# Attention on one core: scaling of two heads of four moved to ScalarE, and one tile per key block for the transposed probabilities

## The chip, the cores and the metric

The kernel runs on one core of a Trainium2 chip. The core has five engines that run their own instruction streams and wait for one another by semaphores: TensorE (PE in the profile; PEld is its loading of weights), VectorE (DVE), ScalarE (ACT), GpSimd (POOL) and SyncE (SP, which issues the DMAs). SBUF is the on-chip memory of 128 partitions; PSUM holds what TensorE writes. The metric is the device time of one execution in microseconds, the median of the runs.

## The reference, cut to what matters

The program is a block of a diffusion transformer: 512 latent tokens and 256 context tokens of width 1024, two layers. Each layer has a mixer (attention, a convolution and a state-space scan side by side, one output projection) and an MLP. Only the attention is touched by the change. It has 8 query heads in 2 groups of 4 (one group for each key head, `kv`), width 64. A block of 128 latent tokens sees itself and its two neighbours, all 256 context tokens, and a "sink" logit that takes part in the sum of the softmax and has no value:

```python
s_lat = jnp.where(mask, jnp.einsum('bqhgd,bkhd->bhgqk', qb, kb) * scale, NEG_INF)
s_ctx = jnp.einsum('bqhgd,bkhd->bhgqk', qb, kc) * scale
p = jax.nn.softmax(jnp.concatenate([s_lat, s_ctx, s_sink], axis=-1), axis=-1)
out = einsum('bhgqk,bkhd->bqhgd', p_lat, vb) + einsum('bhgqk,bkhd->bqhgd', p_ctx, vc)
```

Context tokens attend to the context alone, and only in the first layer (layer 0), since the second layer (layer 1) has no context output.

## The kernel before, in words

All large products are float32 products made of three passes on TensorE (`mm3`, L640 to L642: high by high, high by low, low by high part), so a weight that comes by DMA is split first, by a cast on ScalarE (L623) and a subtraction on VectorE or GpSimd (L624).

The attention stage is `phase_a`. After keys, values and queries it walks over units. A unit is one tile of 128 tokens and one `kv`, that is four heads. Layer 0 has 12 units: four of context tokens with 2 key blocks (256 columns of scores), then eight of latent tokens, the first and the last two with 4 key blocks (512 columns), the other four with 5 (640 columns). Layer 1 has the eight latent units alone. For each unit:

- `attn_scores`: for each of the four heads TensorE makes the scores (L932 to L935) in a PSUM tile `ps_q` (two buffers), and VectorE adds the mask and takes the maximum while it writes them to an SBUF tile `p` (L936). Then small steps on VectorE (L940, L941), the exponential of the sink on ScalarE (L942), the exponential of each head on ScalarE with the row sum beside it (L944), the sum and its reciprocal on VectorE (L946, L947), and at last the scaling of each head's `p` by the reciprocal: four instructions on VectorE (L949).
- `attn_values`: for each key block `j` TensorE transposes that block of the four heads (L962) into one PSUM tile `ps_t` (two buffers, shared by the transposes, the products with the values and the query transposes L905). The block is copied to SBUF, into `pts`, by ScalarE for even `j` (L569 is the line of the helper `E.copy`) and by VectorE for odd `j` (L963). `pts` is one tile for all blocks of a unit, with one buffer. Then the products with the values (L969, two for each block), a cast of the result on ScalarE (L972) and a subtraction on VectorE (L973) into the tiles that the output projection reads.

`values` of a unit is written one unit behind its `scores`. Between units TensorE gets other work: query transposes for the next units (L905, with L910 and L911 behind them) and the first pass of the output projection (`pass0`, copied by ScalarE at L1357, multiplied by GpSimd at L1359). After the attention comes `phase_post` with the second pass, the normalisation (L587 to L606, L732) and the modulation before the MLP (L782 to L787).

What sets the order: the kernel is written with a tile framework that is told `schedule_with_timeline_sim=True`. It simulates the engines and sets the order of each engine's instructions by its simulated times. So an edit of an instruction's engine or of a tile's buffers changes the order of others too, also away from the edit. On the chip each engine then runs its stream strictly in that order.

Of the kernel before, what the change touches and what calls it, by code (L numbers as in the profile page):

```python
# [7 lines left out]
F32 = mybir.dt.float32  # L8
# [4 lines left out]
OP = mybir.AluOpType  # L13
AX = mybir.AxisListType

P = 128
# [898 lines left out]
def attn_scores(E, blk, kv, qs, lat, kt):  # L915

    nc = E.nc
    V = nc.vector
    keys = ([k for k in (blk - 1, blk, blk + 1) if 0 <= k < 4] if lat else []) + [4, 5]
    nk = len(keys)  # L920
    nl = nk - 2
    moff = {0: 1, 1: 0, 2: 0, 3: 5}[blk] if lat else 3
    p = [E.p3([P, 5 * P]) for _ in range(4)]
    st = E.sm.tile([P, 4, 4], F32, name="st", tag="st", bufs=4)
    mx, nm, sm, es = (st[:, k] for k in range(4))
    for i in range(4):
        pq = E.pt('q')
        l0 = 512 - nl * P
        qi = qs[:, i // 2, i % 2]
        if nl:  # L930
            rk = slice(keys[0] * P, (keys[0] + nl) * P)
            nc.tensor.matmul(pq[:, l0:512], qi, kt[0][:, kv, rk], start=True, stop=False)  # L932
            nc.tensor.matmul(pq[:, l0:512], qi, kt[1][:, kv, rk], start=False, stop=True)
        nc.tensor.matmul(pq[:, 512:768], qi, kt[0][:, kv, NL:], start=True, stop=False)
        nc.tensor.matmul(pq[:, 512:768], qi, kt[1][:, kv, NL:], start=False, stop=True)  # L935
        V.tensor_tensor_reduce(out=p[i][:, :nk * P], in0=pq[:, l0:768],  # L936
                               in1=E.mask[:, moff:moff + nk].rearrange("p a b -> p (a b)"), scale=0.125,
                               scalar=-3e38, op0=OP.add, op1=OP.max, accum_out=mx[:, i:i + 1])
    h4 = slice(kv * 4, kv * 4 + 4)
    V.scalar_tensor_tensor(out=nm, in0=mx, scalar=-1.0, in1=E.nsink[:, h4], op0=OP.mult, op1=OP.min)  # L940
    V.tensor_sub(es, nm, E.nsink[:, h4])  # L941
    nc.scalar.activation(es, es, AF.Exp)  # L942
    for i in range(4):
        nc.scalar.activation(p[i][:, :nk * P], p[i][:, :nk * P], AF.Exp, bias=nm[:, i:i + 1],  # L944
                             accum_out=sm[:, i:i + 1])
    V.tensor_add(sm, sm, es)  # L946
    V.reciprocal(sm, sm)  # L947
    for i in range(4):
        V.tensor_scalar(out=p[i][:, :nk * P], in0=p[i][:, :nk * P], scalar1=sm[:, i:i + 1], scalar2=None,  # L949
                        op0=OP.mult)  # L950
    return p, keys


def attn_values(E, kv, p, keys, v, mix):
    nc = E.nc
    V = nc.vector
    nk = len(keys)
    pts = E.ap.tile([P, 5, 512], F32, name="pts", tag="pts", bufs=1)
    for j in range(nk):
        pt = E.pt('t')  # L960
        for i in range(4):
            nc.tensor.transpose(pt[:, i * P:(i + 1) * P], p[i][:, j * P:(j + 1) * P], E.ident)  # L962
        (V.tensor_copy if j % 2 else E.copy)(pts[:, j], pt)  # L963
    po = E.pt('t')
    for j in range(nk):
        vv = v[:, keys[j], kv * 64:(kv + 1) * 64]
        pr = pts[:, j].rearrange("p (a e t) -> p a e t", a=2, e=2)
        for e in range(2):
            nc.tensor.matmul(po[e * 64:(e + 1) * 64, :256], vv, pr[:, :, e], start=j == 0, stop=j == nk - 1)  # L969
    pv = po[:, :256].rearrange("p (a t) -> p a t", a=2)  # L970
    mh, ml = mix(0), mix(1)
    nc.scalar.copy(mh, pv)  # L972
    V.tensor_sub(ml, pv, mh.bitcast(F32))  # L973
# [275 lines left out]
def phase_a(E, l, cols, st):  # L1249
# [115 lines left out]
    def values():  # L1365
        (i0, t0, kv0), pk0 = pend.pop(0)
        ts = slice((t0 % 4) * P, (t0 % 4 + 1) * P)

        def mix(q):
            return mAl[q][kv0][:, :, ts] if t0 < 4 else mAc[q][:, kv0 * 2:kv0 * 2 + 2, ts]  # L1370

        attn_values(E, kv0, *pk0, vt, mix)
        return kv0 == 0 and i0 >= E.plag[l]

    for n, u in enumerate(units):
        i, t, kv = u
        while nq < len(order) and nq <= (n + E.qa[l]) // 2:
            q_proj(order[nq])
            nq += 1
        while len(qss) < min(len(units), n + 1 + E.nqs - 2):  # L1380
            qss.append(attn_q(E, units[len(qss)][2], q_all[units[len(qss)][1]]))
        p0 = len(pend) >= E.vlag and E.vfirst and values()
        pend.append((u, attn_scores(E, t % 4, kv, qss[n], t < 4, kt)))
        p0 = p0 or (len(pend) > E.vlag and values())
        if p0:
            pass0(done)
            done += 1
# [343 lines left out]
```

## Time and profile before

| | us |
|---|---|
| median of 3 runs (lowest, highest) | 1626.89 (1626.73, 1628.28) |
| the profiled execution | 1627.44 |
| its span, from the first instruction to the last | 1625.7 |
| PE busy in the span | 1522.6 (94%) |
| DVE busy | 1078.5 (66%) |
| ACT busy | 639.2 (39%) |
| POOL busy | 188.0 (12%) |

The mean granted clock of TensorE is 0.967 of full speed. A busy share says how long an engine had something to do; the rows further down say where TensorE had nothing to do, and what ended that. In the timeline rows a bracket stands behind the first instruction after an idle time: how long the engine sat idle, and which instruction of which engine released it. A row of windows has the start and end, the length, the busy time and number of instructions of PE, PEld, DVE, ACT and POOL, and then the granted clock, the share of the DMA engines and GB/s.

### The profile page before, as it was taken

The numbers are of one execution on the slowest core, as the hardware profiler recorded it, in microseconds if no ns is written. First come the engines' busy times: TensorE is split into PE (matmuls) and PEld (weight loads), VectorE is DVE, ScalarE is ACT, GpSimd is POOL, SyncE is SP. The second block draws the span as 40 slices with busy tenths as digits, with TensorE's granted clock in tenths as the row PEclk, the third lists the DMA queues.
The fourth block names the chain that finished last, engine by engine and source line by source line (L and its number), as shares of the span: only waits on it lengthen the run. The fifth ranks groups of instructions, "written<-read, shape, count | busy, mean of one in ns | idle before, by whom it ended". The sixth has DMA issues, their size and how long they took to land.

```text
span 1625.7 us, 22752 instructions
## 1 busy us (share of the span) xinstructions
PE 1522.6 (94%) x8740; PEld 1232.8 (76%) x8740; DVE 1078.5 (66%) x2288; ACT 639.2 (39%) x1199; POOL 188.0 (12%) x185
## 2 busy tenths in 40 slices
PE   5899999899999999999999997999889799999997
PEld 2677776667888888887888875688677688888885
DVE  8766638667885472647466476563763878879785
ACT  5411235654523121443334344122463564445441
POOL 0000121002312110000000135003201100000012
PEclk9999999999999999999999998879999899999999
DMA  9366412005232253042230347743302243232312
GB/s 346 120 209 207 151 46 79 1 21 187 73 134 93 76 178 100 29 132 102 106 130 2 121 186 295 266 143 93 117 1 104 104 155 104 89 119 85 123 59 84
DMA packets 72765, 193.82 MB, mean 119 GB/s; under 512 B 14928, under 2 KB 25424, under 8 KB 72272
## 3 DMA queue, kind: packets, MB, share of 16 engines
q1 hardware_dynamic: 68208, 188.17, 33.3%
q10 hardware_dynamic: 4448, 4.19, 0.8%
q8 instruction: 69, 1.13, 0.3%
q14 instruction: 40, 0.33, 0.1%
HBM read 172.15 MB, written 20.19 MB: 118 GB/s over the span
## 4 chain that ended last, share of the span: by engine, by line
PE 79%; DVE 11%; DMA 4%; ACT 4%; issue 1%; SPq 0%; POOL 0%; DVEq 0%; ACTq 0%
PE ps_m L640 15%; PE ps_m L641 15%; PE ps_m L642 15%; PE ps_q L1507 4%; PE ps_q L1508 4%; PE ps_q L1509 4%; PE ps_a L827 3%; PE ps_q L641 3%; PE ps_q L640 3%; PE ps_q L642 3%; ACT p L944 2%; PE ps_s L526 2%; DVE p L936 1%; PE ps_t L969 1%; DVE p L949 1%
## 5 line engine op out<-in xcount | busy, mean ns | idle before, releaser
L623 ACT CAST w<-w 128x1024 fp32r<-128x1024 f32 x128 | 133.8, 1049 | 221.6 <-PE ps_q L641 72.5
L641 PE MATMUL ps_m<-g,w 128*128 128x256 f32 (+1 forms) x544 | 178.6, 330 | 0.0
L640 PE MATMUL ps_m<-g,w 128*128 128x256 f32 (+1 forms) x544 | 177.0, 330 | 1.2 <-DVE g L784 1.2
L624 POOL TENSOR_TENSOR w<-w 128x1024 fp32r<-128x1024 f32 x33 | 80.6, 2443 | 839.4 <-ACT w L623 411.9
L642 PE MATMUL ps_m<-g,w 128*128 128x256 f32 (+1 forms) x544 | 177.5, 328 | 0.0
L641 PE MATMUL ps_m<-f,w 128*128 128x512 f32 (+1 forms) x464 | 170.0, 367 | 0.3 <-POOL f L787 0.3
L642 PE MATMUL ps_m<-f,w 128*128 128x512 f32 (+1 forms) x464 | 170.2, 368 | 0.0
L640 PE MATMUL ps_m<-f,w 128*128 128x512 f32 (+1 forms) x464 | 170.2, 371 | 0.0
L624 DVE TENSOR_TENSOR w<-w 128x1024 fp32r<-128x1024 f32 x95 | 120.1, 1267 | 74.8 <-ACT w L623 68.2
L640 PE MATMUL ps_m<-w,f 128*128 128x512 f32 (+1 forms) x400 | 147.6, 373 | 8.9 <-DVE p L989 4.0
L642 PE MATMUL ps_m<-w,f 128*128 128x512 f32 (+1 forms) x400 | 147.7, 370 | 0.0
L641 PE MATMUL ps_m<-w,f 128*128 128x512 f32 (+1 forms) x400 | 146.8, 368 | 0.0
L1516 DVE TENSOR_TENSOR g<-g,ps_q 128x512 f32<-128x512 f32 x146 | 93.4, 681 | 31.3 <-PE ps_q L1509 30.9
L641 PEld LDWEIGHTS ps_m<-g,w 128*128 128x128 f32 x544 | 104.0, 191 | 11.2 <-issue 1.2
L640 PEld LDWEIGHTS ps_m<-g,w 128*128 128x128 f32 x544 | 103.2, 192 | 11.7 <-DVE g L784 1.5
L642 PEld LDWEIGHTS ps_m<-g,w 128*128 128x128 f32 x544 | 103.8, 191 | 9.5 <-DVE w L624 0.4
L640 PEld LDWEIGHTS ps_m<-f,w 128*128 128x128 f32 x464 | 88.8, 193 | 19.6 <-issue 6.2
L642 PEld LDWEIGHTS ps_m<-f,w 128*128 128x128 f32 x464 | 88.9, 192 | 17.7 <-issue 4.5
L641 PEld LDWEIGHTS ps_m<-f,w 128*128 128x128 f32 x464 | 88.8, 191 | 14.6 <-DVE ssm_tab L303 1.2
L640 PEld LDWEIGHTS ps_m<-w,f 128*128 128x128 f32 x400 | 75.9, 190 | 22.7 <-issue 3.6
L640 PE MATMUL ps_q<-w,f 128*128 128x512 f32 x224 | 87.7, 395 | 2.3 <-DVE g L1682 2.0
L641 PE MATMUL ps_q<-w,f 128*128 128x512 f32 x224 | 87.8, 393 | 0.0
(319 smaller groups left out, 3256.3 us busy)
## 6 DMA issues: line engine op xcount, KB each, us to landing
w<-in_w_ada SPq DMA_DIRECT2D x72, 512.0 KB
w<-in_w_mlp_in SPq DMA_DIRECT2D x64, 512.0 KB
w<-in_w_mlp_out SPq DMA_DIRECT2D x36, 512.0 KB
wr<-in_w_mlp_out SPq DMA_DIRECT2D x14, 1024.0 KB
ada_w<-in_w_ada SPq DMA_DIRECT2D x21, 512.0 KB
w<-in_w_out SPq DMA_DIRECT2D x16, 512.0 KB
w<-in_w_conv SPq DMA_DIRECT2D x12, 512.0 KB
h_d<-g SPq DMA_DIRECT2D x12, 512.0 KB
```

The lines of the kernel that those rows point to most:

```text
L526: nc.tensor.matmul(out(g), U[d].o[rows, q, k].rearrange("p t i -> p (t i)"), sp[d][rows, q, k, lo:NCH], start=False, stop=d == 1 and q == ...
L623: nc.scalar.copy(hi, raw)
L624: (nc.gpsimd if turn % 2 and E.wpool and pool else nc.vector).tensor_sub(lo, raw, hi.bitcast(F32))
L640: nc.tensor.matmul(out, lh, rh, start=first, stop=False)
L641: nc.tensor.matmul(out, lh, rl, start=False, stop=False)
L642: nc.tensor.matmul(out, ll, rh, start=False, stop=last)
L827: nc.tensor.matmul(pa[32 * b:32 * b + 32, k * 256:(k + 1) * 256], E.cT[:, kc], raw[k][:, b * 256:(b + 1) * 256], start=kc == 0 and k == 0, ...
L944: nc.scalar.activation(p[i][:, :nk * P], p[i][:, :nk * P], AF.Exp, bias=nm[:, i:i + 1], accum_out=sm[:, i:i + 1])
L1507: nc.tensor.matmul(o, f[:, 0, c, js], rh[:, c], start=first and c == 0, stop=False, **kw)
L1508: nc.tensor.matmul(o, f[:, 0, c, js], rl[:, c], start=False, stop=False, **kw)
L1509: nc.tensor.matmul(o, f[:, 1, c, js], rh[:, c], start=False, stop=c == 1, **kw)
L1516: V.tensor_add(a_, a_, b_)
```

## The change

It has two edits. In `attn_scores` heads 1 and 3 of a unit are scaled by ScalarE (a multiplication by a column of reciprocals, line 950 of the kernel after), heads 0 and 2 by VectorE as before. In `attn_values` the transposed probabilities get a tile of 512 columns for each key block, in a ring of nine places, where one tile with one buffer held up to five blocks. What is computed is the same.

```diff
@@ attn_scores
     for i in range(4):
-        V.tensor_scalar(out=p[i][:, :nk * P], in0=p[i][:, :nk * P], scalar1=sm[:, i:i + 1], scalar2=None,
-                        op0=OP.mult)
+        if i % 2:
+            nc.scalar.mul(p[i][:, :nk * P], p[i][:, :nk * P], sm[:, i:i + 1])
+        else:
+            V.tensor_scalar(out=p[i][:, :nk * P], in0=p[i][:, :nk * P], scalar1=sm[:, i:i + 1], scalar2=None,
+                            op0=OP.mult)
@@ attn_values
-    pts = E.ap.tile([P, 5, 512], F32, name="pts", tag="pts", bufs=1)
+    pts = []
     for j in range(nk):
         pt = E.pt('t')
         for i in range(4):
             nc.tensor.transpose(pt[:, i * P:(i + 1) * P], p[i][:, j * P:(j + 1) * P], E.ident)
-        (V.tensor_copy if j % 2 else E.copy)(pts[:, j], pt)
+        pts.append(E.ap.tile([P, 512], F32, name="pts", tag="pts", bufs=9))
+        (V.tensor_copy if j % 2 else E.copy)(pts[j], pt)
     po = E.pt('t')
     for j in range(nk):
         vv = v[:, keys[j], kv * 64:(kv + 1) * 64]
-        pr = pts[:, j].rearrange("p (a e t) -> p a e t", a=2, e=2)
+        pr = pts[j].rearrange("p (a e t) -> p a e t", a=2, e=2)
```

Four lines are added, so what stood at L949, L962, L963, L969, L972 and L973 stands at L952, L965, L967, L973, L976 and L977 after; L950 is the new one. In the rows below `p_` with a number is one head's tile of probabilities; the numbers differ between the two kernels.

The order on ScalarE in layer 1, where its first two units meet (their heads are p_10439 to 10442 and p_10525 to 10528 before, p_10471 to 10474 and p_10560 to 10563 after). Before:

```order
L944 ACTIVATE p_10527,st<-p_10527,st 128x512
L942 ACTIVATE st<-st 128x4
L944 ACTIVATE p_10528,st<-p_10528,st 128x512
L569 COPY pts<-ps_t 128x512 x2
L972 CAST f_10326<-ps_t 128x2x128
```

The same place on ScalarE after:

```order
L944 ACTIVATE p_10562,st<-p_10562,st 128x512
L942 ACTIVATE st<-st 128x4
L944 ACTIVATE p_10563,st<-p_10563,st 128x512
L950 ACTIVATE p_10472<-p_10472,st 128x512
L950 ACTIVATE p_10474<-p_10474,st 128x512
L950 ACTIVATE p_10561<-p_10561,st 128x512
L950 ACTIVATE p_10563<-p_10563,st 128x512
L569 COPY pts<-ps_t 128x512 x2
L976 CAST f_10358<-ps_t 128x2x128
```

Four scalings, two of each unit, stand between the last exponential of the second unit and the first copy of the first.

The order on ScalarE in layer 0 at the second and third unit, both of context tokens (the second unit's last two heads are p_2574 and p_2575 before, p_2575 and p_2576 after; the third unit begins with p_2665 before, p_2667 after). Before:

```order
L944 ACTIVATE p_2575,st<-p_2575,st 128x256
L942 ACTIVATE st<-st 128x4
L569 COPY pts<-ps_t 128x512
L972 CAST f_2372<-ps_t 128x2x128
L910 CAST qs<-ps_t 64x2x128 x2
L569 COPY pts<-ps_t 128x512
L944 ACTIVATE p_2665,st<-p_2665,st 128x256
```

The same place on ScalarE after:

```order
L944 ACTIVATE p_2576,st<-p_2576,st 128x256
L942 ACTIVATE st<-st 128x4
L569 COPY pts<-ps_t 128x512
L944 ACTIVATE p_2667,st<-p_2667,st 128x256
L950 ACTIVATE p_2574<-p_2574,st 128x256
L950 ACTIVATE p_2576<-p_2576,st 128x256
L944 ACTIVATE p_2668,st<-p_2668,st 128x256
L942 ACTIVATE st<-st 128x4
L944 ACTIVATE p_2669,st<-p_2669,st 128x256
L944 ACTIVATE p_2670,st<-p_2670,st 128x256
L976 CAST f_2372<-ps_t 128x2x128
```

The cast of the first unit's result (L972, now L976) has moved behind all exponentials of the third unit and two scalings of the second. The first unit's own two scalings stand earlier, between two casts and exponentials.

The order on TensorE at the end of the attention of layer 1, in the last unit (p_11096 to 11099 before, p_11153 to 11156 after), among the matmuls of the output projection's first pass. Before:

```order
L640 MATMUL ps_m<-w,f_10326 128x512
L641 MATMUL ps_m<-w,f_10326 128x512
L962 MATMUL ps_t<-ident,p_11096 128x128
L962 MATMUL ps_t<-ident,p_11097 128x128
L962 MATMUL ps_t<-ident,p_11098 128x128
L962 MATMUL ps_t<-ident,p_11099 128x128
L642 MATMUL ps_m<-w,f_10328 128x512
L640 MATMUL ps_m<-w,f_10326 128x512
```

The same place on TensorE after:

```order
L640 MATMUL ps_m<-w,f_10358 128x512
L641 MATMUL ps_m<-w,f_10358 128x512
L965 MATMUL ps_t<-ident,p_11153 128x128
L965 MATMUL ps_t<-ident,p_11154 128x128
L965 MATMUL ps_t<-ident,p_11155 128x128
L965 MATMUL ps_t<-ident,p_11156 128x128
L965 MATMUL ps_t<-ident,p_11153 128x128
L965 MATMUL ps_t<-ident,p_11154 128x128
L965 MATMUL ps_t<-ident,p_11155 128x128
L965 MATMUL ps_t<-ident,p_11156 128x128
L642 MATMUL ps_m<-w,f_10360 128x512
L640 MATMUL ps_m<-w,f_10358 128x512
```

The transposes of the third key block have moved ahead of four matmuls of the projection.

## Rows read from the trace of the kernel before

**Rows 1.** Windows, both attentions: start:end, length, then as told above.

```profile
236.00:366.00 130.00, 117.18 (x708) 88.74 (x708) 91.98 (x260) 71.86 (x188) 18.30 (x15) 0.96 0.10 32
1152.00:1238.00 86.00, 75.47 (x484) 57.24 (x484) 61.38 (x160) 48.74 (x122) 7.63 (x5) 0.96 0.12 44
```

**Rows 2.** What PE waited for, layer 0's attention: us, times, longest.

```profile
PE ps_t L962 <- DVE pts L963: 2.4, 5, 0.8
PE ps_t L969 <- ACT pts L569: 2.0, 5, 0.7
```

**Rows 3.** The same, layer 1; then L969's line (busy us, mean ns | idle).

```profile
PE ps_q L932 <- DVE st L936: 4.3, 5, 1.7
PE ps_t L962 <- DVE pts L963: 2.5, 4, 0.8
...
L969 PE MATMUL ps_t<-pts,vt 128*64 128x256 f32 x144 | 18.4, 388 | 3.2 <-ACT pts L569 2.0 <-DVE pts L963 1.1
```

**Rows 4.** What ACT waited for most, layer 0's attention, then layer 1's.

```profile
ACT f L972 <- PE ps_t L969: 26.4, 10, 3.7
...
ACT f L972 <- PE ps_t L969: 20.7, 7, 4.4
```

**Rows 5.** Lines by form (busy us, mean ns | idle), layer 0; L1207's durations.

```profile
L944 ACT ACTIVATE p<-p,st 128x640 f32<-128x640 f32 x16 | 13.1, 819 | 1.0 <-DVE st L940 0.9
...
L949 DVE TENSOR_SCALAR p<-p,st 128x640 f32<-128x640 f32 x16 | 8.8, 611 | 0.1
...
L949 DVE TENSOR_SCALAR p<-p,st 128x512 f32<-128x512 f32 x16 | 6.7, 480 | 0.1
...
L949 DVE TENSOR_SCALAR p<-p,st 128x256 f32<-128x256 f32 x16 | 5.2, 381 | 0.1
...
L1207 ACT ACTIVATE f<-f,vecs x6: 510/722/723, 110.8 to 1061.1; 128x512 f32<-128x512 f32 x4, 128x256 f32<-128x256 f32 x2
```

**Rows 6.** Timeline, layer 1's first two units: ACT, DVE, PE.

```profile
1160.05 0.71 ACT L944 ACTIVATE p<-p,st 128x512 f32<-128x512 f32 x1
...
1160.88 0.58 ACT L569 COPY pts<-ps_t 128x512 f32<-128x512 f32 x1
...
1158.25 1.68 DVE L949 TENSOR_SCALAR p<-p,st 128x512 f32<-128x512 f32 x4
...
1161.52 1.09 PE L962 MATMUL ps_t<-ident,p 128*128 128x128 f32 x8 [0.72 <-ACT pts L569]
...
1164.97 0.45 PE L932 MATMUL ps_q<-kt,qs 128*128 128x384 f32 x1 [0.61 <-DVE st L936]
```

**Rows 7.** Timeline, layer 0's first three units: ACT, PE.

```profile
256.14 0.58 ACT L569 COPY pts<-ps_t 128x512 f32<-128x512 f32 x1
259.41 0.38 ACT L972 CAST f<-ps_t 128x256 fp32r<-128x256 f32 x1 [2.69 <-PE ps_t L969]
...
256.24 0.58 PE L934 MATMUL ps_q<-kt,qs 128*128 128x256 f32 x1 [1.09 <-DVE st L936]
...
261.19 0.63 PE L962 MATMUL ps_t<-ident,p 128*128 128x128 f32 x4 [0.41 <-DVE f L973]
```

**Rows 8.** Timeline, PE's stalls behind scalings: first and last of seven.

```profile
273.27 0.39 PE L932 MATMUL ps_q<-kt,qs 128*128 128x256 f32 x1 [0.75 <-DVE st L936]
...
1212.04 1.08 PE L969 MATMUL ps_t<-pts,vt 128*64 128x256 f32 x8 [0.38 <-DVE pts L963]
```

**Rows 9.** Timeline, a scaling beside GpSimd: DVE, POOL.

```profile
334.76 2.95 DVE L949 TENSOR_SCALAR p<-p,st 128x640 f32<-128x640 f32 x4
...
335.47 1.43 POOL L1359 TENSOR_TENSOR f<-f,f 128x512 f32<-128x512 f32 x1 [20.70 <-ACT dump L719]
```

**Rows 10.** Timeline, PE at both attentions' ends: first and last of seven stalls.

```profile
356.49 1.95 PE L969 MATMUL ps_t<-pts,vt 128*64 128x256 f32 x16 [0.29 <-ACT pts L569]
...
1238.83 0.50 PE L640 MATMUL ps_m<-w,f 128*128 128x512 f32 x1 [0.80 <-ACT f L972]
```

**Rows 11.** Timeline, PE after layer 0's attention, before the MLP.

```profile
404.40 0.38 PE L640 MATMUL ps_m<-g,w 128*128 128x256 f32 x1 [1.24 <-DVE g L784]
```

## The prediction

> **What bounds the kernel now.** I read the windows first. In both attentions together TensorE is busy 192.7 of 216 us, VectorE 153.4, ScalarE 120.6 [rows 1]. TensorE is the bound there, as in the whole span, but it idles 12.8 us in layer 0 and 10.5 us in layer 1 (window less busy). These 23.3 us are all that the change can win directly; 20 us taken from a VectorE that is not the bound are worth only what of them ends an idle time of TensorE.
>
> Next I read the waits of TensorE. They are many and short, and both engines that the change touches end them: VectorE's block copies 2.4 and 2.5 us in nine stalls, its masks 4.3 us in layer 1, and ScalarE's block copies 2.0 and 2.0 us, five stalls in each layer [rows 2, 3]. So a gain on VectorE is real and so is a price on ScalarE. Then ScalarE's own waits: 26.4 and 20.7 us in 17 spells before L972 [rows 4]. There it sits until the products with the values come; that is the room in which new work costs nothing, if it is ready at that time.
>
> **What leaves VectorE and comes to ScalarE.** Each unit has four scalings of 381, 480 or 611 ns for 256, 512 or 640 columns [rows 5]. Layer 0 has four units of each width, layer 1 four of 512 and four of 640. Two of four go: 8 x (0.38 + 0.48 + 0.61) = 11.8 us in layer 0 and 8 x (0.48 + 0.61) = 8.7 us in layer 1, 20.5 us less on VectorE. The trace has no such scaling on ScalarE. The nearest row is an activation of 510 ns at 256 and 722 ns at 512 columns (L1207); for 640 the exponential's 819 ns is the bound above, and VectorE's own times the bound below [rows 5]. I take L1207's, as it also reads and writes SBUF with one operand per partition: 8 x (0.51 + 0.72 + 0.82) + 8 x (0.72 + 0.82) = 28.7 us more on ScalarE. ScalarE then has some 149 of 216 us, VectorE some 133: both below TensorE. So the sum is one of places, not of totals.
>
> The Trainium skill ("Perfetto Trace Analysis", section "Optimizing Scalar/DVE Operations") speaks against this change: where VectorE has a fast mode it is the faster engine, and moving work to ScalarE makes sense if VectorE is saturated. The rows agree on the first half (0.48 against 0.72 us) and show a VectorE that is busy 71% of the two windows, not full; by that rule the edit costs time, up to the 28.7 - 20.5 = 8.2 us of added work if all of it lay on the path, 1635.1 us.
>
> **Gains.** (1) Later units: seven stalls of TensorE that VectorE ends stand right behind a row of scalings, from 0.75 us at 273.27 to 0.38 us at 1212.04, 3.74 us together [rows 8]. Two scalings fewer end 0.96 to 1.2 us earlier, which covers each; but heads 1 and 3 now come from ScalarE, and a transposed block needs all four. I take two thirds, -2.5 us (0 to -3.7). One of these rows of four took 2.95 us because a GpSimd multiplication of 1.43 us ran across it [rows 9]; with two instructions there is less to collide. The Trainium skill ("SBUF — State Buffer", section "Who interferes with whom") says that VectorE and GpSimd share a port pair under an exclusive lock and that ScalarE has ports of its own; the trace agrees for VectorE. By that rule about 1 us of VectorE's time returns at each collision, which the term above already holds.
> (2) Layer 0's first units: the mask that ends the 1.09 us at 256.24 stands behind four scalings of 256 columns [rows 7]. Two of 381 ns go, overlapped some 0.6 us in all: -0.6 us (0 to -1.1).
> (3) The ends of both attentions: there, with the places for blocks, the order moves transposes ahead of projection matmuls. Seven stalls stand there, from 0.29 us at 356.49 to 0.80 us at 1238.83, 4.0 us together [rows 10]. Only those that wait for a block copy can profit, and the projection matmuls that were cover are used up earlier: -1.0 us (0 to -2.0).
> The nine places in themselves I cost at nothing: in no row does a block copy wait for the products with the values to give its place back, and copies wait for transposes. They act through the order alone.
>
> **Losses.** (4) Layer 1's first two units. VectorE finished the first unit's four scalings 1.68 us after 1158.25, and ScalarE began its first block copy at 1160.88, right behind the last exponential (1160.05 + 0.71) [rows 6]. In the new order four scalings stand between: two of 512 columns for each unit. Four of VectorE's took 1.68 us where their means add to 1.92; by that ratio four of 722 ns take 2.5 us, so the copy begins at about 1163.3, 2.4 us later. Behind it wait the transposes of the third block (1161.52) and then the scores at 1164.97, which had 0.6 us of waiting for VectorE; VectorE is now early, so that much is absorbed. +1.8 us. With VectorE's 0.48 us as price it is +1.2, with ScalarE's 0.82 us +2.6.
> (5) Layer 0's context units. ScalarE has copied the first unit's first block by 256.72 and is idle 2.69 us before L972 at 259.41 [rows 7]. In the new order two scalings and all four exponentials of the third unit come ahead of L972: six by about 0.51 us, overlapped some 2.7 us. They would just fit, but cannot start at once, since the third unit's masks are made on VectorE at that time. What waits behind L972 is VectorE's L973, and behind it TensorE's transposes at 261.19, already the last to be ready by 0.41 us. These exponentials are then done earlier than before, which gives part back: +1.0 us (0 to +2.7).
> (6) Later units: ScalarE's copies that stand behind two scalings. Ten stalls of TensorE already end with such a copy [rows 2, 3]. A copy that follows two scalings of 0.6 us could come 1.2 us late; mostly the scalings fall into the idle spells before L972 and the copies were done. +1.0 us (0 to +6, which is 0.6 us at each of the ten).
> (7) Elsewhere the schedule moves some steps: before layer 0's MLP a cast (L784) that ends a stall of 1.24 us now comes earlier on VectorE's queue [rows 11], but behind a weight subtraction; in layer 1 a store and a few steps swap. Zero, from -1.2 to +0.8, and as an allowance 1.5 us either way for small swaps in other stages.
>
> **The sum.** -2.5 - 0.6 - 1.0 + 1.8 + 1.0 + 1.0 + 0 = -0.3 us. The profiled execution took 1627.44 us (1625.7 of span and 1.74 around it), 0.55 us above the median of the runs; 1626.89 - 0.3 gives 1626.6 us. A measurement of this kernel can tell about 0.2% from no change, 3.3 us; this lies within.
>
> **Rivals.** *Faster, about 1619.4 us.* All scalings on ScalarE fall into its 47 us of idle spells [rows 4], the first units cost nothing, and a third of TensorE's 23.3 us goes: -7.5 us. For it speaks that VectorE's stalls are more than ScalarE's [rows 2, 3]; against it that ScalarE's spells begin after its copies are done, while the scalings must come before the next unit's copies.
> *Slower, about 1634 us.* ScalarE's queue becomes the late one. It serves exponentials, scalings and even blocks' copies in strict order, so each copy that TensorE waits for stands behind scalings of another unit. Price: +2.6 at (4), +2.7 at (5), +6 at (6), less 4.1 of gains (1) to (3): +7.2 us. It decides this way from the point where a unit's scalings end after its predecessor's transposes, so that ten stalls grow by 0.6 us each; (4) shows that order in the instructions themselves. The skill's rule above points to this case.
> *It does not do what it says, 1627 us.* Relief on VectorE is hidden behind ScalarE at every place, the places free nothing, and the same TensorE stalls end with another engine's name.
>
> **How the numbers follow.** Chances: my sum 0.42, faster 0.30, slower 0.20, no effect 0.08. The sum's own range is 1622 to 1631 us (its terms' ends added with mixed signs), so a little of it lies past 0.2% on either side. Faster by over 0.2% (below 1623.6): 0.30 + 0.05 = 0.35. Slower (above 1630.1): 0.20 + 0.05 = 0.25. Within: 0.40. All ends together would give 1618.6 (every gain, with loss (4) at its least) and 1640.5 (every loss, no gain). For 8 in 10 I reach to the two rivals, below with the allowance of 1.5 us: 1618 to 1634 us.
>
> **What would show it.** Right: VectorE some 20 us less busy and ScalarE 25 to 30 us more; the rows of scalings on ScalarE at 0.5 to 0.8 us; TensorE's waits for VectorE's copies and masks shorter by 3 us and its waits for ScalarE's copies longer by 2 to 4; the transposes of layer 1's first unit waiting some 2.5 us for a ScalarE copy. Wrong: waits for ScalarE's copies unchanged (then (4) to (6) cost nothing and the time is near 1620), or grown past 8 us (then it is near 1634); a scaling on ScalarE far from 0.72 us; or a large shift outside the two attentions, where the schedule alone would be the cause.

## The result: slower by 0.7%

| | kernel before | changed kernel |
|---|---|---|
| median of 5 runs, us | 1627.88 | 1638.25 |
| lowest and highest, us | 1626.73, 1630.09 | 1636.78, 1644.86 |
| ratio, 95% interval | | 1.0072 (1.0053 to 1.0092) |
| span of the profiled execution, us | 1625.7 | 1635.0 |

The forecast was 1626.6 us, "within 0.2%", with a range of 1618 to 1634: the time lies above the range. The changed kernel was timed once more on another chip (run e8 below): 1.006 (1.0037 to 1.0084).

The first part of the page of the changed kernel (busy time, share of the span, number of instructions):

```profile
span 1635.0 us, 22756 instructions
...
PE 1526.5 (93%) x8740; PEld 1234.6 (76%) x8740; DVE 1064.3 (65%) x2248; ACT 664.3 (41%) x1239; POOL 188.9 (12%) x185
```

TensorE does the same work. VectorE lost 14.2 us, not the 20.5 of the working, and ScalarE got 25.1 us, not 28.7. The working added the means of single scalings, but neighbours overlap: on VectorE a row of four of 512 columns took 1.67 us and the pair that is left takes 0.88. The scalings themselves, by form over layer 0's attention (the answers to [rows 5]):

```profile
L950 ACT ACTIVATE p<-p,st 128x640 f32<-128x640 f32 x8 | 6.2, 821 | 1.9 <-DVE st L947 1.9
L952 DVE TENSOR_SCALAR p<-p,st 128x640 f32<-128x640 f32 x8 | 6.1, 807 | 0.1
L950 ACT ACTIVATE p<-p,st 128x512 f32<-128x512 f32 x8 | 5.3, 716 | 0.9 <-DVE st L947 0.9
L950 ACT ACTIVATE p<-p,st 128x256 f32<-128x256 f32 x8 | 3.6, 500 | 0.5 <-DVE st L947 0.5
```

On ScalarE a scaling takes 821, 716 and 500 ns, as estimated. On VectorE the 640-column form went from a mean of 611 to 807 ns: two of the four pairs ran beside a GpSimd multiplication and took 2.05 and 2.03 us, where the other two took 1.02; in the kernel before one row of four did so [rows 9]. The windows of both attentions (columns as in [rows 1]; layer 1's is 8 us later):

```profile
236.00:366.00 130.00, 113.92 (x691) 86.28 (x691) 82.53 (x228) 85.80 (x210) 15.66 (x11) 0.95 0.10 33
1160.00:1248.00 88.00, 75.39 (x483) 55.84 (x482) 53.35 (x140) 59.88 (x137) 5.52 (x5) 0.98 0.12 43
```

In the same 130 us TensorE is busy 3.3 us less than in [rows 1] (with 691 matmuls in the window, not 708): its idle time grew from 12.8 to 16.1 us, although VectorE has 9.5 us less to do.

**Where the time went, by stage.** Every matmul of the changed trace was matched with the same one in the trace of before, and its start compared. The table gives how much later (+) or earlier (-) the matmuls became over each stretch, in us; the stretches are named by the time in the trace of before. e8 is a second profile of the changed kernel, e1 one with the order of before.

| stretch | what is there | changed | e8, same program | e1, order of before |
|---|---|---|---|---|
| to 250 | up to the first scores | -4.9 | +2.3 | -2.8 |
| 250 to 262 | layer 0's first context units | +3.3 | +3.5 | 0.0 |
| 262 to 365 | layer 0's other units | +1.5 | +1.6 | +0.1 |
| 365 to 985 | after layer 0's attention, MLP | +0.8 | +1.6 | -0.3 |
| 985 to 1152 | start of layer 1 | +5.6 | -0.2 | -0.1 |
| 1152 to 1170 | layer 1's first two units | +2.2 | +3.4 | -1.0 |
| 1170 to 1240 | layer 1's other units | -0.4 | -0.4 | 0.0 |
| 1240 to the end | after layer 1's attention, MLP | +1.9 | +2.4 | +0.4 |

Two stretches differ by 6 to 7 us between two executions of one program, so nothing is read from them here: the one up to 250 us and the one from 985 to 1152 us (e6 comes back to the second). The others return within 1.2 us, and together make +9.3 and +12.1 us; the medians differ by 10.4.

**Three new stalls** stand behind these numbers. The first is in layer 0's context units (timeline of the changed kernel, ScalarE and then TensorE):

```profile
256.12 0.19 ACT L942 ACTIVATE st<-st 128x4 f32<-128x4 f32 x1
...
256.70 0.49 ACT L944 ACTIVATE p<-p,st 128x256 f32<-128x256 f32 x1
...
257.19 0.34 ACT L976 CAST f<-ps_t 128x256 fp32r<-128x256 f32 x1
...
257.59 0.80 PE L640 MATMUL ps_m<-w,f 128*128 128x512 f32 x1 [2.31 <-ACT f L976]
```

The cast of the first unit's result ran only when the third unit's exponentials were done, and TensorE, which had no other work in its order, sat for 2.31 us. In [rows 7] that cast ran as soon as its products were there, and TensorE went into the same projection matmuls without a wait (the kernel before, then the second of them in the changed kernel):

```profile
259.84 0.70 PE L640 MATMUL ps_m<-w,f 128*128 128x512 f32 x1
260.38 0.40 PE L641 MATMUL ps_m<-w,f 128*128 128x512 f32 x1
...
258.19 0.63 PE L641 MATMUL ps_m<-w,f 128*128 128x512 f32 x1
```

The second of them took 0.40 us before and 0.63 us behind the stall. The granted clock was 0.93 from 260 to 262 us in the kernel before and 0.50 from 258 to 260 us in the changed one. From the L640 to the next scores the same matmuls took 2.75 us before, with 0.41 of idle time in it, and 3.49 us now (3.58 in e8), so about 0.7 us of the loss came behind the stall, beside a lower clock.

The second is in layer 1's first two units (ScalarE, TensorE):

```profile
1166.38 2.55 ACT L950 ACTIVATE p<-p,st 128x512 f32<-128x512 f32 x4
1168.95 0.59 ACT L569 COPY pts<-ps_t 128x512 f32<-128x512 f32 x1
...
1167.14 1.05 PE L965 MATMUL ps_t<-ident,p 128*128 128x128 f32 x6 [2.16 <-ACT p L950]
1168.98 1.97 PE L965 MATMUL ps_t<-ident,p 128*128 128x128 f32 x8 [0.78 <-DVE pts L967]
```

This is the place of [rows 6], and the four scalings came as forecast, in 2.55 us between the last exponential and the first copy. TensorE, however, did not wait for the copy but one step earlier: the first unit's transposes need its heads 1 and 3, whose scalings stand behind all four exponentials of the second unit. The third was not forecast. It is in layer 0's later units (ScalarE, VectorE, TensorE):

```profile
291.36 0.37 ACT L910 CAST qs<-ps_t 64x256 fp32r<-64x256 f32 x1
291.94 0.83 ACT L944 ACTIVATE p<-p,st 128x640 f32<-128x640 f32 x1 [0.21 <-DVE st L940]
...
293.57 0.81 ACT L944 ACTIVATE p<-p,st 128x640 f32<-128x640 f32 x1
...
294.50 0.37 ACT L910 CAST qs<-ps_t 64x256 fp32r<-64x256 f32 x1
...
294.90 0.43 DVE L911 TENSOR_TENSOR qs<-ps_t,qs 64x256 fp32r<-64x256 f32 x1 [2.36 <-ACT qs L910]
...
295.48 1.09 PE L965 MATMUL ps_t<-ident,p 128*128 128x128 f32 x4 [2.21 <-DVE qs L911]
```

In the kernel before the two query casts (L910) of this unit ran ahead of the exponentials:

```profile
293.02 0.36 ACT L910 CAST qs<-ps_t 64x256 fp32r<-64x256 f32 x1
294.03 0.37 ACT L910 CAST qs<-ps_t 64x256 fp32r<-64x256 f32 x1 [0.64 <-DVE qs L911]
294.42 0.83 ACT L944 ACTIVATE p<-p,st 128x640 f32<-128x640 f32 x1
```

Now the second stands behind three exponentials; over the kernel this happens to four query casts, two in each layer, and in the kernel before to none. VectorE's L911 waits 2.36 us for it and holds a place of `ps_t` so long, and TensorE's transposes wait 2.21 us for that place. Layer 1 has the same with 1.4 us.

**What did not grow** are TensorE's waits for ScalarE's block copies (L569), which the forecast's terms (4) and (6) and its slower rival rest on. The changed kernel, layer 0 and then layer 1:

```profile
PE ps_m L640 <- ACT f L976: 3.7, 2, 2.3
PE ps_t L965 <- DVE qs L911: 2.2, 1, 2.2
...
PE ps_t L965 <- ACT pts L569: 0.3, 1, 0.3
PE ps_t L973 <- ACT pts L569: 0.3, 1, 0.3
...
PE ps_t L965 <- ACT p L950: 2.2, 1, 2.2
PE ps_t L965 <- ACT pts L569: 0.8, 1, 0.8
```

They fell from 2.6 to 0.6 us in layer 0 and from 2.7 to 0.8 us in layer 1, and e8 has the same sums (0.6 and 0.8). The loss went through a result cast, query casts and scalings.

### The profile page after: what moved, and what is told of

Same layout as the page of the kernel before. It is cut to its first block, busy times and chain, and to the rows that moved or that the text cites. A ratio compares the mean times of both kernels' runs of the same rounds, so it can differ in the third digit from the quotient of the medians.

```text
span 1635.0 us, 22756 instructions
## 1 busy us (share of the span) xinstructions
PE 1526.5 (93%) x8740; PEld 1234.6 (76%) x8740; DVE 1064.3 (65%) x2248; ACT 664.3 (41%) x1239; POOL 188.9 (12%) x185
## 4 chain that ended last, share of the span: by engine, by line
PE 76%; DVE 12%; ACT 5%; DMA 5%; issue 2%; POOL 0%; SPq 0%; DVEq 0%; ACTq 0%
PE ps_m L640 15%; PE ps_m L641 15%; PE ps_m L642 14%; PE ps_q L1511 4%; PE ps_q L1512 4%; PE ps_q L1513 4%; PE ps_q L640 3%; PE ps_q L641 3%; PE ps_q L642 2%; PE ps_t L973 2%; PE ps_a L827 2%; DMA w<-in_w_ada 2%; ACT p L944 2%; PE ps_s L526 2%; PE ps_t L965 2%
## 5 line engine op out<-in xcount | busy, mean ns | idle before, releaser
L640 PE MATMUL ps_m<-g,w 128*128 128x256 f32 (+1 forms) x544 | 178.0, 331 | 0.0
L640 PE MATMUL ps_m<-f,w 128*128 128x512 f32 (+1 forms) x464 | 171.0, 373 | 0.0
L640 PE MATMUL ps_m<-w,f 128*128 128x512 f32 (+1 forms) x400 | 147.7, 373 | 11.6 <-ACT f L976 5.1
L640 PEld LDWEIGHTS ps_m<-g,w 128*128 128x128 f32 x544 | 104.2, 193 | 10.7 <-ACT relu L1481 0.3
L640 PEld LDWEIGHTS ps_m<-f,w 128*128 128x128 f32 x464 | 89.1, 194 | 21.1 <-issue 7.4
L640 PEld LDWEIGHTS ps_m<-w,f 128*128 128x128 f32 x400 | 76.1, 190 | 25.5 <-ACT f L976 7.7
L640 PE MATMUL ps_q<-w,f 128*128 128x512 f32 x224 | 87.6, 395 | 2.3 <-DVE g L1686 2.0
```

The costliest lines, as they stand in the source:

```text
L640: nc.tensor.matmul(out, lh, rh, start=first, stop=False)
```

## The experiments

Two theories stood against each other at first. **Q**: the price is ScalarE's strict order, at the first units of each layer above all. **O**: the price is the other order that the scheduler chose away from the attention, above all from 985 to 1152 us. Each run below was timed beside the kernel before on the same chip; "late" is meant as in the table of stretches.

### e1: the nine places alone

```diff
-    pts = E.ap.tile([P, 5, 512], F32, name="pts", tag="pts", bufs=1)
+        pts.append(E.ap.tile([P, 512], F32, name="pts", tag="pts", bufs=9))
```

> The nine places alone, all scalings on VectorE. The order of every engine is that of the kernel before. Theory Q (the scalings wait in ScalarE's queue and their readers with them) and theory O (the scheduler's other order away from the attention costs the time) both expect no change, 1627 to 1629 us. A theory P, that the places themselves give back waits or take some, expects more than 3 us of difference. The drift of its trace against the trace of before, stage by stage, shows how far equal instructions wander from one execution to the next.

Ratio 0.9997 (0.9979 to 1.0014). The places do nothing, neither by waits nor by the order: the order of all engines is that of the kernel before, and from 250 to 1100 us its matmuls keep their distance to those of before within 0.4 us. So the whole loss comes with the scaling on ScalarE, and the reordering at the attentions' ends, which the prediction put down to the places, is that of the scaling too.

### e2, e3, e4: the scaling on ScalarE in a part of the units

```diff
-        if i % 2:
+        if i % 2 and split:
```

with `split` true for layer 0's context units and layer 1's first two units (e2), for layer 0 (e3), for layer 1 (e4).

> Scalings on ScalarE in layer 0's four context units and in layer 1's first two units alone; nine places; all other units scale on VectorE. The order changes only inside the attentions and after layer 1's. Q: the price of the first units, +2.6 us at layer 0's (259 us) and +2.2 at layer 1's (1159 us) as in the changed kernel, so about 1632 us. O: no reordering between the attentions, so no loss there and at most 1629 us.

> Scalings on ScalarE in layer 0 alone. All of the reordering between the attentions is there, layer 1's attention scales on VectorE. Q: the changed kernel's trace is 5.4 us late over layer 0's attention, so about 1633 us. O: that and the 5.4 us between 990 and 1150 us as well, about 1636 to 1638 us, with layer 1's own 2.8 us gone.

> Scalings on ScalarE in layer 1 alone. Nothing is reordered before layer 1's attention. Q: 2.8 us over layer 1's attention, about 1631 us. O: at most that and 1 us after the attention; the stage between 990 and 1150 us as before.

| run | ratio (95%) | 250-262 | 262-365 | 365-985 | 1152-1170 | 1170-1240 | 1240-end |
|---|---|---|---|---|---|---|---|
| e2 first units | 1.0050 (1.0033 to 1.0068) | +3.5 | -0.5 | +0.3 | +2.5 | -0.3 | +1.0 |
| e3 layer 0 | 1.0020 (1.0003 to 1.0037) | +3.5 | +1.7 | +1.1 | -1.0 | 0.0 | +0.8 |
| e4 layer 1 | 1.0019 (1.0002 to 1.0035) | 0.0 | +0.1 | -0.3 | +2.4 | -0.4 | +1.8 |

Each loss is there where the scaling of its units is on ScalarE, and only there. The first units alone bring 1.005, more than either layer's whole; 6.5 of these 8.1 us are in the six stretches. One point of e2's expectation does not hold: TensorE's order from 985 to 1100 us is not that of the kernel before in e2, so e2 does not part Q from O there. e3 has all of the changed kernel's order between the attentions and was expected at 1636 to 1638 us by O; its median is 1633.8, against 1629.8 of before. That speaks against O as far as that stretch goes.

### e5: the complement of e2

```diff
+        pend.append((u, attn_scores(E, t % 4, kv, qss[n], t < 4, kt, t < 4 and (both or n > 1))))
```

The last argument is `split`; `t < 4` are the latent tiles, and `both` stands for layer 0.

> The complement of the run on the first units: layer 0's context units and layer 1's first two units scale on VectorE, all other units have heads 1 and 3 on ScalarE; nine places. Q (the price is ScalarE's queue at the first units): no loss at 262 us and at 1162 us, 1 to 2 us over layer 0's later units as in the changed kernel, nothing over layer 1's; ratio to before about 1.001. O (the other order away from the attention costs too): the stage from 985 to 1150 us is ordered as in the changed kernel, so another 3 to 5 us there; ratio 1.003 to 1.004.

Ratio 1.0020 (1.0000 to 1.0041). Nothing at 262 us (-0.1), and -1.0 at 1170 us as in e1, which does not touch that place. Over layer 0's later units +2.2 us, with the stall of 2.2 us at L911 in its waits. Over layer 1's later units -2.2 us: here, with the first units left alone, the units gain, which fits VectorE's relief (one trace).

### e6: an edit that does nothing

```diff
+    if extra:
+        dm = E.sm.tile([P, 4], F32, name="dm", tag="dm", bufs=1)
+        nc.scalar.copy(dm, sm)
```

`extra` is true for layer 0's last unit.

> The kernel before with one more instruction: a ScalarE copy of four columns (about 0.2 us, nobody reads it) in the last unit of layer 0's attention. The order of both attentions stays as before, but the scheduler orders the stage from 1020 to 1140 us in another way, about as in the changed kernel. O: a change of 2 to 4 us in that stage, ratio 1.001 to 1.003. Q: no change, ratio 1.000.

Ratio 0.9994 (0.9976 to 1.0012). The stage from 1020 to 1140 us is ordered in another way, and nothing is lost. Reordering at that place is not in itself a cost.

All traces together say the same. In ten of them TensorE's order from 985 to 1100 us is not that of the kernel before (the changed kernel, e8, e2, e3, e5, e6, e7, e9, e11, e13): from 985 to 1125 us they are between 2.3 us earlier and 4.4 us later, 0.4 us later in the mean. In the five with the order of before (e1, e4, e10, e12, e14) it is -0.3 to +0.6 us. So another order there spreads the executions and costs nothing that shows in the mean.

### e8: the changed kernel again

> The changed kernel once more, for its trace: how far does one program wander from one execution to the next, stage by stage. Q and O: the losses at 262 us (3.4 us), at 1162 us (1.7 us) and over layer 0's later units (1.5 us) return within 0.5 us; the stage from 985 to 1150 us, where the clock drops after idle times, may differ by 2 us. Ratio 1.006 to 1.008.

Ratio 1.0060 (1.0037 to 1.0084); its stretches are in the table of the result. The loss at 262 us and over the later units came back within 0.2 us, the one at 1170 us was 1.2 us larger, and the one from 985 to 1152 us did not come back at all.

### e7, e9, e12: the same work in a forced order

An order was forced by a dependency without a wait, from a unit's exponentials to an instruction that is to stand ahead of them on ScalarE:

```diff
+        for y in behind:
+            E.tc.add_manual_dep(x, y.name, mybir.DependencyInfo(mybir.DependencyClass.NoSync,
+                                                                mybir.DependencyReason.DATA), reason="pin")
```

In e7 `behind` holds the first unit's cast (L976) for layer 0's third unit, and the first unit's scaling for layer 1's second. In e9 it holds the last query cast (L910), for all units. e12 has all three.

> The changed kernel with two orders on ScalarE forced: layer 1's second unit starts its exponentials behind the first unit's two scalings, and layer 0's third unit starts its exponentials behind the cast of the first unit's result (L976). Q: TensorE's stall of 2.3 us that ends with L976 in layer 0 goes, the one of 2.2 us that ends with the scalings in layer 1 goes or shrinks to 1.3; 2 to 4 us less than the changed kernel. If the work on ScalarE itself is the price and not its order, both stalls return under another name and the time stays within 1 us of the changed kernel.

> The changed kernel with one order forced on ScalarE: a unit's exponentials stand behind all query casts (L910) that are written before them, as they did in the kernel before. Theory Q now says that layer 0's later units lose because a query cast slipped behind three exponentials, so that its reader L911 ends a stall of 2.2 us at 295 us and one of 1.4 us in layer 1: both go, 2 to 3.5 us less than the changed kernel; the stalls of the first units (2.3 and 2.2 us) stay. If the later units lose by ScalarE's load and not by this order, the stalls come back with another name and the gain is under 1 us.

> The changed kernel with all three orders forced: query casts ahead of exponentials, layer 0's third unit behind the first unit's cast, layer 1's second unit behind the first unit's scalings. Q: what is left is the work itself on ScalarE at the first units and the order behind the attentions: about half of the changed kernel's loss, ratio 1.002 to 1.004. If the load alone is the price, 1.006 as the changed kernel.

| run | ratio (95%) | 250-262 | 262-365 | 365-985 | 1152-1170 | 1170-1240 | 1240-end |
|---|---|---|---|---|---|---|---|
| changed kernel | 1.0072 (1.0053 to 1.0092) | +3.3 | +1.5 | +0.8 | +2.2 | -0.4 | +1.9 |
| e7 | 1.0043 (1.0026 to 1.0060) | +1.5 | +1.3 | +1.0 | +1.6 | -0.5 | +2.2 |
| e9 | 1.0018 (1.0003 to 1.0033) | +1.3 | +0.4 | +1.4 | +1.4 | -1.3 | +2.3 |
| e12 | 1.0028 (1.0008 to 1.0047) | +1.4 | +0.9 | +1.3 | +0.8 | -1.4 | +2.6 |

TensorE's largest waits in e9 from 236 to 300 us and then from 1150 to 1176 us (what it waited for, us in total, times, longest):

```profile
PE ps_q L932 <- DVE st L936: 1.7, 2, 1.1
PE ps_q L934 <- DVE st L950: 1.3, 1, 1.3
PE ps_m L640 <- ACT f L979: 1.1, 2, 0.6
...
PE ps_q L932 <- DVE st L936: 3.1, 4, 1.7
PE ps_t L968 <- ACT p L953: 1.9, 1, 1.9
```

(That kernel has three lines more from here on: L979, L953 and L968 are the cast L976, the scaling L950 and the transposes L965 of the changed kernel, and its L950 is the reciprocal L947.) The wait for L911 is gone from both, and the one of 2.3 us for the cast shrank to 0.5: with the query casts first, the third unit's exponentials come later and the cast no longer stands behind them. The wait for the scalings in layer 1 stayed, at 1.9 us. So most of the loss in layer 0 is the order of ScalarE's queue: from 250 to 365 us the same 24 scalings cost 1.7 us with the query casts at their old place, where the two traces of the changed kernel have 4.8 and 5.1. For the whole kernel the ratio falls from 1.0072 and 1.0060 to 1.0018, and the six stretches from 9.3 and 12.1 us to 5.5, about half. Of these 5.5 us, 3.7 lie behind the two attentions. e12, with more forced, is not better than e9; the intervals overlap. In layer 1's first units forcing the order returned little: in e7 the stall of 2.16 us went, and the transposes then waited 1.6 us for a copy. There ScalarE's work before the first transposed blocks seems to be the price, whichever part of it comes first.

### e10, e11: only the units of 640 columns

`split` is true for the four units of 640 columns, in layer 1 alone (e10) or in both layers (e11), with the query casts first.

> Heads 1 and 3 on ScalarE only in layer 1's four units of 640 columns, with the query casts ahead of the exponentials; the order away from that attention is that of the kernel before. Q: VectorE's relief gives TensorE some of the 2.2 us back that the run on the later units showed over layer 1's later units; ratio 0.998 to 1.000. If relief of VectorE is worth nothing at all, 1.000; if ScalarE's load costs at any unit, above 1.001.

> The same in both layers: heads 1 and 3 on ScalarE in the four units of 640 columns of each layer, query casts ahead of the exponentials. Layer 0's other units scale on VectorE. Q: no loss at 262 us and 1162 us, layer 0's later units within 1 us of the kernel before, layer 1's 1 to 2 us earlier; ratio 0.998 to 1.001.

e10: 0.9994 (0.9982 to 1.0006), e11: 1.0024 (1.0007 to 1.0041). Even where no first unit is touched and the order behind the attention stays, nothing is gained that can be measured; in layer 0 (+1.2 us from 262 to 365) it costs. No version beat the kernel before.

### e13, e14: relief alone, load alone

```diff
-        if i % 2:
-            nc.scalar.mul(p[i][:, :nk * P], p[i][:, :nk * P], sm[:, i:i + 1])
-        else:
+        if i % 2 == 0:
```

```diff
             nc.scalar.mul(p[i][:, :nk * P], p[i][:, :nk * P], sm[:, i:i + 1])
+            w = E.ap.tile([P, 5 * P], F32, name="w2", tag="w2", bufs=2)
+            V.tensor_scalar(out=w[:, :nk * P], in0=p[i - 1][:, :nk * P], scalar1=sm[:, i:i + 1], scalar2=None,
+                            op0=OP.mult)
```

> VectorE's relief without ScalarE's load: heads 1 and 3 are not scaled at all (this part of the computation is left out), heads 0 and 2 on VectorE; nine places. If the forecast's gains (1) to (3) are there and only outweighed, 4 us less than before, ratio 0.997 to 0.998, most of it where VectorE ended stalls. If relief of VectorE is worth nothing because other things are late there, ratio 0.999 to 1.001; the attention of layer 1 showed -0.4 us over the later units in the changed kernel.

> ScalarE's load without VectorE's relief: heads 1 and 3 are scaled on ScalarE as in the changed kernel, and VectorE in addition writes two scaled copies of heads 0 and 2 that nobody reads, so that it does as much as before; six places, since the copies need the room. The order away from the attentions is that of the kernel before, and in layer 1 nearly so. Q: the loss is ScalarE's order at the first units and is there without any relief, +3 us at 262 us and +3 us at 1160 us, ratio 1.004 to 1.006. If the loss came from the order that VectorE's shorter queue lets the scheduler choose, the ratio is near 1.001.

| run | ratio (95%) | in us | 250-262 | 262-365 | 365-985 | 1152-1170 | 1170-1240 | 1240-end |
|---|---|---|---|---|---|---|---|---|
| e13 relief | 0.9982 (0.9967 to 0.9997) | -2.9 | -0.5 | +1.6 | 0.0 | -2.0 | -0.7 | 0.0 |
| e14 load | 1.0051 (1.0033 to 1.0069) | +8.3 | +0.4 | +5.4 | +4.2 | +2.6 | -0.2 | +1.0 |

e14 also has six places in place of nine, for room. Gain and loss are both there. Relief is worth 2.9 us (0.5 to 5.4), though the scheduler put the query cast behind the exponentials in e13 as well: its largest wait from 236 to 366 us is that one again (the transposes are L963 there, VectorE's copy L965).

```profile
PE ps_t L963 <- DVE qs L911: 2.2, 1, 2.2
PE ps_t L963 <- DVE pts L965: 1.6, 2, 0.8
```

Load is worth 8.3 us (5.4 to 11.2). In e14 the expected loss at 262 us did not come (+0.4), since the order there was another; it came later, where VectorE's block copies and L911 end the waits from 236 to 366 us (transposes L968, copy L970):

```profile
PE ps_t L968 <- DVE pts L970: 3.3, 3, 1.7
PE ps_t L968 <- DVE qs L911: 2.7, 2, 2.2
```

So the stall of layer 0's first units belongs to one particular order, but load without relief was as dear under another order. The +4.2 us of e14 behind layer 0's attention are not the load's: they come from 430 to 500 us, where TensorE's order is that of the kernel before and the granted clock was 0.83 from 420 to 440 us, against 1.00 from 415 to 435 us there; this trace is also the slowest of e14's nine executions. In layer 1's first units the loss came without any relief (+2.6 us). The two add to 5.4 us, less than the 10.4 of the changed kernel; the intervals leave 4 us open either way. Whether relief and load simply add is not shown.

## Why the prediction was wrong, point by point

The sum failed at the order of ScalarE's queue: it priced the scalings where they stood and took the query casts beside them as unmoved. The slower rival was right in kind (ScalarE's strict order makes others late) and wrong in its sum: its +7.2 us had ten stalls at ScalarE's copies grow by 0.6 us each, and these waits fell by 3.9 us. That its 1634 us came nearest is in part luck. By the forecast's terms, the measured ones from the two traces of the changed kernel:

- **(1), (3) and (6), later units, together -2.5 us.** Measured +1.5 and +1.6 us in layer 0, -0.4 in both traces in layer 1: +1.1 us. The gains were there, as e13 (-2.9 us in all) and layer 1 in e5 (-2.2 us) show; the stall of 0.75 us at 273.27 [rows 8] is gone. (6) had the wrong instruction: not block copies but the query cast came late. The working followed the scalings through ScalarE's queue and took all other instructions as standing where they were. The order of the changed kernel had L910 behind three exponentials, and it was there to be read. e9 shows it: 1.1 us of the 1.5 return over these units, and more at others.
- **(2) and (5), layer 0's first units, together +0.4 us.** Measured +3.3 and +3.5. The place and the chain (six instructions ahead of L972, then what waits for it) were named rightly; the size was not, and it is above even the upper bound of 2.7. Matmul by matmul the 3.3 us are: the mask's matmul 0.5 us earlier, about as (2) has it; the products behind it 0.7 us later, with a wait of 0.61 us for a mask; the projection's matmul 2.4 us later, for the cast; and 0.7 us behind that, beside the lower clock (e8: -0.5, +0.7, +2.5 and +0.8). The working looked for who waits behind L972 and took VectorE's L973 and the transposes at 261.19. It overlooked that TensorE's next projection matmul reads the cast itself, and that nothing else stood in TensorE's order at that time: 2.31 us for it alone.
- **(4), layer 1's first units, +1.8 us.** Measured +2.2 and +3.4; the four scalings took 2.55 us against 2.5 in the working. The place and the size were right, the step was not: TensorE waited 2.16 us (2.29 in e8) for the first unit's own scalings and not for the copy behind them, which is partly luck.
- **(7), elsewhere, zero.** Measured +0.8 and +1.6 behind layer 0's attention and +1.9 and +2.4 behind layer 1's, where e1 has -0.3 and +0.4. The stall of 1.24 us [rows 11] did go, but others came: TensorE's wait for L976 at the end of each attention grew from 0.8 us [rows 10] to 1.4, and the one for L745 behind layer 1's from 9.8 to 10.7. It goes with the order: behind layer 1's attention the traces of the tables whose TensorE order there is not that of the kernel before (the changed kernel, e8, e4, e7, e9, e12) have +1.8 to +2.6, the five others (e1, e2, e3, e13, e14) 0.0 to +1.0. So theory O holds for some 1.5 us there. Which of the reordered steps is the cause was not tried one by one and stays open.
- **The nine places** were costed at nothing, and e1 agrees. That the reordering at the ends came with them, as term (3) has it, was wrong.
- **The signs.** As forecast: a scaling on ScalarE at 0.50 to 0.82 us, ScalarE 25.1 us busier. Not as forecast: TensorE's waits for ScalarE's copies, longer by 2 to 4 us by the forecast, were 3.9 us shorter. The working read unchanged waits as a time near 1620 us; they fell and the time rose, since casts and scalings were left out of that sign.
- **The Trainium skill's two rules.** The Trainium skill ("Perfetto Trace Analysis", section "Optimizing Scalar/DVE Operations") says that moving work to ScalarE may make sense where VectorE is saturated. With VectorE busy 71% of the windows the edit cost 10.4 us, in the direction that the prediction drew from it and above the 8.2 us of added work that the prediction took as its most. The Trainium skill ("SBUF — State Buffer", section "Who interferes with whom") has VectorE and GpSimd share a port pair under an exclusive lock. The prediction expected two instructions to collide less than four; in layer 0 two of four pairs of 640 columns took 2.05 and 2.03 us against 1.02, where before one row of four did, so this loss grew from 1.0 to 2.0 us.
- **Range and chances.** 0.25 stood on slower, and the range ended at 1634. All losses together had been worked out as 1640.5; the range left the upper part out, because the terms' ends were added with mixed signs. The losses did not come singly: the new order moved four query casts and a result cast together.

## What to carry to other kernels

Before work is moved to an engine that has room, read what that engine's queue holds between two hand-overs, not its busy share: here ScalarE was 56% busy in the attentions, and what came to stand in front of one cast or scaling stalled TensorE by 1.4 to 2.3 us at a time. Where a scheduler sets the order, compare every row of the changed order near a hand-over with the one before, also those of instructions that the edit does not name, and then force the few that matter: the query casts put back at their place cut the loss from 0.6 or 0.7% to 0.2%. Relief and load can be measured apart, by leaving the moved work out and by doing it on both engines; that says whether there was anything to win (here 2.9 us of 1629).

## What the runs showed of the hardware

After the same idle time TensorE's clock did not always fall. From 1132 to 1136 us TensorE is busy 1.1 of 4 us in the kernel before and waits 2.9 us for VectorE at the end of it; every trace here has this wait (3.9 us in e11). The stretch behind it, from 1138 to 1140 us, in the kernel before and in e4, whose order is the same up to there (columns as in [rows 1]):

```profile
1138.00:1140.00 2.00, 2.00 (x11) 1.65 (x10) 0.00 (x0) 0.00 (x0) 1.63 (x2) 1.00 0.00 0
```

```profile
1138.00:1140.00 2.00, 2.00 (x6) 1.52 (x6) 0.00 (x0) 0.00 (x0) 1.86 (x2) 0.50 0.00 0
```

The granted clock is 1.00 in the one (2.4 GHz) and 0.50 in the other (1.2 GHz), with 11 and 6 matmuls in the same 2 us. It cost 1.3 to 1.8 us from 1100 to 1152 us in most of the runs (2.5 in e11) and nothing in e1 and e13. So such a difference between single traces need not be the kernel's.

Over whole executions the mean granted clock is lower in the changed kernel: 0.961 to 0.968 in the six of e8, with a median of 0.9645, against a median of 0.969 in the 27 of the kernel before beside them. It does not follow the loss alone: e9 and e12 have 0.9655 with a ratio of 1.002 to 1.003. No run parts what the stalls cost by themselves from what a lower clock behind them adds.
